# Which engine reads the score banks: ACT copies both halves of the scores to SBUF, and DVE adds and bounds them there

## Chip, cores and metric

One core of a Trainium2 chip runs the whole kernel. The metric is the device time of one execution in microseconds; 901.45 us is the median of three runs before the change.

## The reference, cut to what matters

One layer of a streaming encoder block on 1024 positions of width 1024: a norm, one input projection, attention in a window, a gated mixing branch, two output projections, a residual and a last norm. The change lies in the attention alone:

```
s = jnp.einsum('bnqhgd,bnkhd->bhgnqk', qc, kb,
               preferred_element_type=jnp.float32) * (HEAD_DIM ** -0.5)
...
m = jnp.maximum(jnp.max(s, axis=-1, keepdims=True), sink)
p = jnp.exp(s - m)
denom = jnp.sum(p, axis=-1, keepdims=True) + jnp.exp(sink - m)
o = jnp.einsum('bhgnqk,bnkhd->bnqhgd', p / denom, vb.astype(jnp.float32))
```

There are 16 heads of 64 channels, two groups of keys, chunks of 64 positions, and 192 keys that a query sees (fewer at the start of the sequence). All in float32.

## The kernel before, in words

**Product matmuls.** Nearly all of TensorE's work is large products, each done with seven half-size products in place of eight (`gemm_pair`), and each float32 operand split into a high and a low part. ACT casts the high part (`split`, L176), DVE subtracts to get the low part (L177), and three matmuls of 128x512 make up each step (`product`, L357). A product of 12 matmuls ends in a bank of PSUM (`ps_mm`, `ps_o` or `ps_tp`); ACT copies some of these into tiles `x` (L375, L379, L382, L527), DVE adds others (L387, L392, L396). Weights come in as `wr` over the sync queue (L212) or as sums `s`; DVE makes further sums of them (L257 to L260).

**Attention between them.** The attention is written as a generator that is advanced by one or two parts behind each product (the `hook` calls in `gemm_pair`), from about 303 to 580 us. There are 32 steps: two key groups, eight tiles of 128 queries, two parities of heads. A step has these parts: turn the weights of the step before last (transposes L1481 into `ps_tp`, split L176/L177 into `pT`, L1500/L1502 into `pTb`), scores of the chunks c = 0, scores of the chunks c = 1, values of an earlier step (L1516, L1521 into `ps_o`, out by L1529 on ACT and L1530 on DVE).

**The scores.** For each c there is a pair of score matmuls (L1433), one for each i. Queries and keys are split in high and low parts too, stacked along the contraction and the columns, so that one matmul of 384 columns gives both halves of the sum for 192 keys: `sc[:, 0, :]` and `sc[:, 1, :]`. The result lies in one of the two banks `ps_sc`. Then ACT copies the second half into the tile `sl` (L1441; two buffers), DVE adds the first half from PSUM to `sl`, writes the sum to `pr`, and keeps its minimum and the bound of the sink in `nmax` (L1442, one custom instruction and a short one that reads its accumulator), and ACT takes the exponential with the row's sum (L1452). After both c, DVE and ACT work out the denominators (L1458 to L1462) and scale (DVE L1467 for c = 0, ACT L1469 for c = 1).

There are 128 score matmuls, 64 pairs: 112 of 384 columns, eight of 256 and eight of 128. A pair needs both banks, so it waits for the last reader of the pair before.

**Order.** Each engine runs its instructions in a fixed order. It is not written out by hand: a scheduler in the framework places every instruction when the program is built, by its own estimates of when operands and banks come free. A change of one reader therefore moves instructions on other engines.

Of the kernel before, what the change touches and what calls it, by code (L numbers as in the profile page):

```python
# [24 lines left out]
F32 = mybir.dt.float32  # L25
# [5 lines left out]
P = 128  # L31
# [21 lines left out]
def hybrid_tile(  # L53
# [16 lines left out]
    nc = tc.nc  # L70
# [12 lines left out]
    def bank(tag, dt=F32):  # L83
        return psum.tile([P, 512], dt, name=nm("ps_" + tag), tag="ps_" + tag, bufs=2)

    def mtile(shape, dt, tag, bufs, pool=None):
        return (pool or main).tile(shape, dt, name=nm(tag), tag=tag, bufs=bufs)
# [1315 lines left out]
    def atile(shape, dt, tag, bufs):  # L1403
        return mtile(shape, dt, tag, bufs, pool)
# [3 lines left out]
    def small():  # L1408
        return mtile([P, 2, 2], F32, "sm", 12, aheads)

    def window_of(t, c):

        return (64 * c, 64 * c + 192) if t else (P, P + 64 * (c + 1))

    def softmax_stage(g, t, par, qt):

        kt = keys[g, t][0]
        q_of = qt[:].rearrange("p i (q c) -> p c (i q)", c=2)  # L1420
        nmax, sums = small(), small()
        n_pr[0] += 1
        pr = mtile([P, 2, 384], F32, f"pr{n_pr[0] % 2}", 1, aheads if n_pr[0] % 2 else weights_pool)
        held_in = {}
        sinks_of = (v[:, 4 * g + par : 4 * g + par + 3 : 2] for v in (sink_sb, nsink_sb))
        sk, nsk = sinks_of
        for c in range(2):
            lo, hi = window_of(t, c)
            wide = hi - lo
            scores = []  # L1430
            for i in range(2):
                sc = bank("sc")[:, 0 : 2 * wide].rearrange("p (f k) -> p f k", f=2)
                nc.tensor.matmul(  # L1433
                    sc, q_of[:, c, i * P : (i + 1) * P], kt[:, :, lo:hi], start=True, stop=True
                )
                scores.append(sc)
            for i, sc in enumerate(scores):
                at = 192 * (1 - c) if t else P * (1 - c)
                held_in[c, i] = v = pr[:, i, at : at + wide]
                by_low = atile([P, 192], F32, "sl", 2)[:, 0:wide]  # L1440
                nc.scalar.copy(by_low, sc[:, 1, :])  # L1441
                nc.vector.tensor_tensor_reduce(  # L1442
                    v,
                    sc[:, 0, :],
                    by_low,
                    1.0,
                    nsk[:, i : i + 1],
                    op0=ALU.add,
                    op1=ALU.min,
                    accum_out=nmax[:, c, i : i + 1],  # L1450
                )
                nc.scalar.activation(  # L1452
                    v, v, AF.Exp, bias=nmax[:, c, i : i + 1], scale=-1.0, accum_out=sums[:, c, i : i + 1]
                )
            if c == 0:
                yield
        es = small()
        nc.vector.tensor_add(es[:], sk.unsqueeze(1).broadcast_to([P, 2, 2]), nmax[:])  # L1458
        nc.scalar.activation(es[:], es[:], AF.Exp)
        nc.vector.tensor_add(es[:], es[:], sums[:])  # L1460
        inv = small()
        nc.vector.reciprocal(inv[:], es[:])  # L1462
        for c in range(2):
            for i in range(2):
                v = held_in[c, i]
                if c == 0:
                    nc.vector.tensor_scalar_mul(v, v, inv[:, c, i : i + 1])  # L1467
                else:
                    nc.scalar.mul(v, v, inv[:, c, i : i + 1])  # L1469
        held.append(pr)  # L1470
        yield
# [66 lines left out]
    def attention():  # L1538
# [14 lines left out]
        for n, step in enumerate(steps):  # L1553
            if n >= 2:
                weigh(n - 2)
                yield
            halves = softmax_stage(*step, qT.pop(0))
            next(halves)
            yield
            next(halves)  # L1560
            if n + 2 < len(steps):
                qT.append(query_stage(*steps[n + 2]))
            if n in (0, 2):
                value_loads(*tiles[n // 2])
            yield
            if n >= 3:
                value(n - 3)
                yield
# [419 lines left out]
    for p in range(4):  # L1988
# [93 lines left out]
        wide = HALF // 2  # L2082
# [98 lines left out]
```

## Time and profile before

| what | value |
|---|---|
| median of 3 runs (lowest to highest) | 901.45 us (901.11 to 903.2) |
| the profiled execution's own time | 901.43 us |
| its span | 899.6 us |
| mean granted TensorE clock | 0.998 |
| instructions | 13022 |
| PE / weight loads / DVE / ACT / POOL busy | 98% / 81% / 76% / 62% / 17% |
| score copy on ACT, L1441 | 128 |
| add and bound on DVE, L1442 | 128, busy 46.7 us |
| exponential on ACT, L1452 | 128, busy 55.9 us |
| score matmuls, L1433 | 128, busy 42.7 us |

The engines are PE (TensorE's matmuls), PEld (its weight loads, which overlap matmuls), DVE, ACT, POOL and SP. An arrow `out<-in` names the tiles that an instruction writes and reads. In tables of waits and groups, what stands behind an idle time is the instruction that ended it. The profiler models when a matmul ends, and successive matmuls overlap, so a stall is read better from the distance of two starts than from gaps between bars.

### The profile page before, as it was taken

The page shows a single profiled execution, that of the slowest core. Times are in us where ns is not written, and L with a number is a line of the kernel's source. Part 1 is how long each engine was busy: PE and PEld are TensorE (multiplying, and loading weights), DVE is VectorE, ACT ScalarE, POOL GpSimd, SP SyncE. Part 2 cuts the span into 40 slices and gives each one's busy share as a digit, 9 for nine tenths or more (in the row PEclk, how much of TensorE's full clock was granted, in tenths as well). Part 3 has the DMA queues.
Part 4 walks back from the last instruction along what each step waited for, and adds up shares of the span by engine and source line. Part 5 has one row for each costly group of instructions (what it writes and reads, how often), then busy time and mean ns, then how long its engine had stood idle before and what let it go on. Part 6 is the DMA issues. An engine that isn't in the chain of part 4 may idle for free.

```text
span 899.6 us, 13022 instructions
## 1 busy us (share of the span) xinstructions
PE 885.8 (98%) x4117; PEld 731.1 (81%) x4117; DVE 686.9 (76%) x1362; ACT 562.2 (62%) x1189; POOL 152.9 (17%) x218
## 2 busy tenths in 40 slices
PE   9999999999999999999999999999999999999997
PEld 6888888888888787888878787888888888888886
DVE  7879966666685778988777888757796478479886
ACT  7875533334445488888778787855586376367443
POOL 3322222212030010111211011100121122110012
PEclk9999999999999999999999999999999999999999
DMA  9998887958778676887776689979899789998523
GB/s 333 220 283 211 271 199 162 182 161 275 249 244 285 190 193 174 215 194 186 163 223 196 224 252 210 241 277 382 289 292 391 282 229 250 314 293 282 190 101 133
DMA packets 130961, 212.38 MB, mean 236 GB/s; under 512 B 12779, under 2 KB 59371, under 8 KB 130893
## 3 DMA queue, kind: packets, MB, share of 16 engines
q1 hardware_dynamic: 108280, 148.36, 49.3%
q0 software_dynamic: 22464, 62.93, 31.2%
q8 instruction: 32, 0.52, 0.2%
q14 instruction: 37, 0.30, 0.1%
q10 hardware_dynamic: 148, 0.27, 0.1%
HBM read 146.37 MB, written 86.11 MB: 258 GB/s over the span
## 4 chain that ended last, share of the span: by engine, by line
PE 77%; DVE 9%; ACT 5%; DMA 4%; issue 3%; SPq 1%; POOL 0%; ACTq 0%; DVEq 0%
PE ps_mm L357 34%; PE ps_o L357 19%; PE ps_tp L357 7%; PE ps_sc L357 3%; PE ps_tp L788 2%; PE ps_o L788 2%; PE ps_mm L788 2%; DMA wr<-in_w_dram 2%; PE ps_sc L1433 2%; PE ps_tp L1104 2%; ACT pr L1452 1%; DVE pr L1442 1%; DVE pTb L1502 1%; PE ps_sc L788 1%; PE ps_tp L1481 1%
## 5 line engine op out<-in xcount | busy, mean ns | idle before, releaser
L176 ACT CAST wh<-s 128x1024 fp32r<-128x1024 f32 (+1 forms) x79 | 79.3, 1005 | 78.5 <-PE ps_mm L357 30.3
L177 DVE TENSOR_TENSOR wl<-wr,wh 128x512 fp32r<-128x512 f32 (+1 forms) x77 | 72.1, 938 | 63.8 <-ACT wh L176 62.9
L177 DVE TENSOR_TENSOR wl<-s,wh 128x1024 fp32r<-128x1024 f32 (+1 forms) x79 | 92.6, 1172 | 11.9 <-ACT wh L176 11.9
L176 ACT CAST wh<-wr 128x512 fp32r<-128x512 f32 (+1 forms) x77 | 63.1, 821 | 61.0 <-PE ps_mm L357 33.4
L1452 ACT ACTIVATE pr<-pr,sm 128x192 f32<-128x192 f32 (+2 forms) x128 | 55.9, 439 | 24.2 <-DVE sm L1442 23.9
L1442 DVE CUSTOM_DVE_ANT_0 pr<-ps_sc,sl,nsink_sb 128x192 f32<-128x192 f32 (+2 forms) x128 | 46.7, 401 | 16.7 <-ACT sl L1441 15.8
L357 PE MATMUL ps_o<-T_t1h,wh 128*128 128x512 f32 x148 | 57.9, 391 | 0.0
L357 PE MATMUL ps_o<-T_t1h,wl 128*128 128x512 f32 x148 | 57.8, 390 | 0.0
L357 PE MATMUL ps_o<-T_t1l,wh 128*128 128x512 f32 x148 | 57.6, 389 | 0.0
L357 PE MATMUL ps_mm<-T_b11h,wh 128*128 128x512 f32 x140 | 55.0, 393 | 0.0
L357 PE MATMUL ps_mm<-T_t3h,wh 128*128 128x512 f32 x140 | 54.9, 392 | 0.0
L357 PE MATMUL ps_mm<-T_t3h,wl 128*128 128x512 f32 x140 | 54.7, 391 | 0.0
L357 PE MATMUL ps_mm<-T_b11l,wh 128*128 128x512 f32 x140 | 54.7, 391 | 0.0
L357 PE MATMUL ps_mm<-T_t2h,wh 128*128 128x512 f32 x140 | 54.7, 390 | 0.0
L357 PE MATMUL ps_mm<-T_t2h,wl 128*128 128x512 f32 x140 | 54.6, 390 | 0.0
L357 PE MATMUL ps_mm<-T_b11h,wl 128*128 128x512 f32 x140 | 54.6, 390 | 0.0
L357 PE MATMUL ps_mm<-T_t3l,wh 128*128 128x512 f32 x140 | 54.6, 390 | 0.0
L357 PE MATMUL ps_mm<-T_t2l,wh 128*128 128x512 f32 x140 | 54.5, 389 | 0.0
L357 PE MATMUL ps_mm<-T_t4h,wh 128*128 128x512 f32 x136 | 53.5, 393 | 0.0
L357 PE MATMUL ps_mm<-T_t4h,wl 128*128 128x512 f32 x136 | 53.1, 391 | 0.0
L357 PE MATMUL ps_mm<-T_t4l,wh 128*128 128x512 f32 x136 | 53.0, 390 | 0.0
L1433 PE MATMUL ps_sc<-k,q 128*128 128x384 f32 (+2 forms) x128 | 42.7, 376 | 5.5 <-DVE sm L1442 4.9
(425 smaller groups left out, 2451.6 us busy)
## 6 DMA issues: line engine op xcount, KB each, us to landing
wr<-in_w_dram SPq DMA_DIRECT2D x86, 256.0 KB
sums<-in_w_dram POOLq DMA_DIRECT2D x20, 512.0 KB, 7.1
s<-sums SPq DMA_DIRECT2D x20, 512.0 KB
q_hl<-qhl SPq DMA_DIRECT2D x16, 512.0 KB
q<-q_hl SPq DMA_DIRECT2D x64, 128.0 KB
y_dr<-x POOLq DMA_DIRECT2D x28, 256.0 KB, 6.4
g<-in_w_dram POOLq DMA_DIRECT2D x12, 512.0 KB, 6.1
wr<-in_w_dram SPq DMA_DIRECT2D x11, 512.0 KB
```

Source lines behind the costliest of these rows:

```text
L176: hi_of.append(nc.scalar.copy(hi, src))
L177: lo_of.append(nc.vector.tensor_sub(lo, src, hi.bitcast(F32)))
L357: nc.tensor.matmul(acc, lt, rt, start=fresh and k == 0 and n == 0, stop=k == 3 and n == 2, skip_group_check=True,)
L788: mm = nc.tensor.matmul(acc[:], lt, rt, start=fresh and k == 0 and n == 0, stop=stops and k == 3 and n == terms[-1], skip_group_check=True,)
L1104: nc.tensor.matmul(pm[:, t * P : (t + 1) * P], xh[:, half * 4 + t, g * P : (g + 1) * P], bias[-1][1][:, g % 4, :], start=True, stop=True,)
L1433: nc.tensor.matmul(sc, q_of[:, c, i * P : (i + 1) * P], kt[:, :, lo:hi], start=True, stop=True)
L1442: nc.vector.tensor_tensor_reduce(v, sc[:, 0, :], by_low, 1.0, nsk[:, i : i + 1], op0=ALU.add, op1=ALU.min, accum_out=nmax[:, c, i : i + 1],)
L1452: nc.scalar.activation(v, v, AF.Exp, bias=nmax[:, c, i : i + 1], scale=-1.0, accum_out=sums[:, c, i : i + 1])
L1481: nc.tensor.transpose(dst, pr[:, i, block * P : block * P + width], ident[:])
L1502: nc.vector.tensor_sub(b[c][sides[1 - c]], pt[sides[c], 0:256], b[c][sides[c]].bitcast(F32))
```

## The change

`sl` gets room for both halves; ACT copies the whole bank's 384 columns into it (256 or 128 at the start of the sequence), and DVE's operation takes both inputs from `sl`. Nothing else in the source changes.

```diff
-                by_low = atile([P, 192], F32, "sl", 2)[:, 0:wide]
-                nc.scalar.copy(by_low, sc[:, 1, :])
+                two = atile([P, 2, 192], F32, "sl", 2)[:, :, 0:wide]
+                nc.scalar.copy(two, sc)
                 nc.vector.tensor_tensor_reduce(
                     v,
-                    sc[:, 0, :],
-                    by_low,
+                    two[:, 0, :],
+                    two[:, 1, :],
                     1.0,
                     nsk[:, i : i + 1],
```

The bank `ps_sc` then has ACT's copy as its only reader, and the scheduler places score matmuls differently. On TensorE, at the product that runs around 418 us of the profile (into the bank ps_mm_4066, by the form T_t3), the pair of score matmuls into ps_sc_4243 and ps_sc_4245 stood inside the product:

```order
 L357 MATMUL ps_mm_4066<-T_t3l_755,wh_4045 128x512
-L1433 MATMUL ps_sc_4243<-k_3922,q_4027 128x384
 L357 MATMUL ps_mm_4066<-T_t3h_754,wl_4046 128x512
-L1433 MATMUL ps_sc_4245<-k_3922,q_4027 128x384
 L357 MATMUL ps_mm_4066<-T_t3h_754,wh_4045 128x512
```

Now both stand ahead of that product, right behind the one before:

```order
 L357 MATMUL ps_o_4223<-T_b21h_142,wl_3897 128x512
+L1433 MATMUL ps_sc_4243<-k_3922,q_4027 128x384
+L1433 MATMUL ps_sc_4245<-k_3922,q_4027 128x384
 L357 MATMUL ps_mm_4066<-T_t3h_754,wh_4045 128x512
 L357 MATMUL ps_mm_4066<-T_t3l_755,wh_4045 128x512
```

The pair moved up by eight product matmuls. The next pair of the same kind, into ps_sc_4341 (around 426 us), moved by five in the same way, and of the 64 pairs 25 begin earlier than before, by one to twelve product matmuls; the others begin at their old place.

On ACT, at the same place of the program, the copies grow and a few neighbours change places (wide copies L1441, the exponentials L1452, the cast of turned weights L176 and L1500, the output copy L1529):

```order
-L1441 COPY sl_4247<-ps_sc_4243 128x192
-L1441 COPY sl_4251<-ps_sc_4245 128x192
+L1441 COPY sl_4247<-ps_sc_4243 128x384
+L1441 COPY sl_4251<-ps_sc_4245 128x384
+L176 CAST pT_4295<-ps_tp_4290 128x512
 L1529 COPY aT_4268<-ps_o_4269 64x2x4x64
 L1452 ACTIVATE pr_789_4210,sm_4209<-pr_789_4210,sm_4208 128x192 x2
-L176 CAST pT_4295<-ps_tp_4290 128x512
```

A pair of copies still stands behind the exponentials of the pair before, and one cast moved ahead of the next exponentials. On DVE the rows of L1442 keep their order and name `sl` as their only tile input beside the bounds; adds next to them change places by one or two. On the sync queue some loads of queries, keys and weights change places; the queue of POOL is the same.

## The prediction

> **What bounds the kernel now.** I read the page's busy shares first, then busy time by stretch, then who waits for whom, then a short piece of the timeline, and last the chain of waits.
>
> ```profile
> PE 885.8 (98%) x4117; PEld 731.1 (81%) x4117; DVE 686.9 (76%) x1362; ACT 562.2 (62%) x1189; POOL 152.9 (17%) x218
> ```
>
> TensorE bounds the whole, and 899.6 - 885.8 = 13.8 us of idle is all that the page grants. The change touches only the score rows, which run from 303 to 580 us. The table of busy time has that stretch and, as a clean one, 600 to 700 us. Its columns are length, then busy time and instructions of PE, PEld, DVE, ACT and POOL, then the granted clock, the DMA share and GB/s.
>
> ```profile
> 303.00:580.00 277.00, 271.46 (x1310) 222.08 (x1308) 224.66 (x646) 223.47 (x680) 38.46 (x49) 1.00 0.76 204
> 600.00:700.00 100.00, 100.00 (x443) 82.81 (x442) 75.74 (x88) 64.29 (x85) 15.50 (x26) 1.00 0.99 344
> ```
>
> The clock is full in both, so it explains nothing. In the score stretch PE idles 5.5 us, DVE is busy 81% and ACT 81% (53.5 us free). The table of waits, from 300 to 600 us, for PE and its weight loads, and from 303 to 580 us for ACT:
>
> ```profile
> PE ps_sc L1433 <- DVE sm L1442: 4.9, 13, 0.9
> PEld ps_sc L1433 <- DVE sm L1442: 14.7, 25, 1.0
> ACT pr L1452 <- DVE sm L1442: 23.9, 23, 2.2
> ACT wh L176 <- PE ps_mm L357: 7.3, 9, 2.0
> ACT aT L1529 <- PE ps_o L1521: 5.4, 9, 1.0
> ACT pr L1469 <- DVE sm L1462: 4.0, 6, 1.5
> ```
>
> PE waits there for one thing: a score matmul needs a bank of ps_sc (there are two), and the last reader of a bank is DVE's add-and-bound at L1442. The loss lies between 4.9 us (matmul idle, understated because the modelled end of one matmul lies beyond the start of the next) and 14.7 us (weight loads). One case in the timeline shows how much is real (start, duration, engine, line, in us):
>
> ```profile
> 415.83 0.53 ACT L1441 COPY sl<-ps_sc 128x192 f32<-128x192 f32 x2
> 418.00 0.39 PE L357 MATMUL ps_mm<-T_t3h,wh 128*128 128x512 f32 x1
> 418.22 0.39 PE L357 MATMUL ps_mm<-T_t3l,wh 128*128 128x512 f32 x1
> 418.45 0.42 DVE L1442 CUSTOM_DVE_ANT_0 pr<-ps_sc,sl,nsink_sb 128x192 f32<-128x192 f32 x1
> 418.93 0.19 PEld L1433 LDWEIGHTS ps_sc<-k,q 128*128 128x128 f32 x1 [0.74 <-DVE sm L1442]
> 418.94 0.45 PE L1433 MATMUL ps_sc<-k,q 128*128 128x384 f32 x1 [0.32 <-DVE sm L1442]
> 419.22 0.39 PE L357 MATMUL ps_mm<-T_t3h,wl 128*128 128x512 f32 x1
> 419.81 0.52 ACT L1441 COPY sl<-ps_sc 128x192 f32<-128x192 f32 x2
> 423.85 0.53 ACT L1441 COPY sl<-ps_sc 128x192 f32<-128x192 f32 x2
> 425.66 0.39 PE L357 MATMUL ps_mm<-T_t4l,wh 128*128 128x512 f32 x1
> 426.02 0.45 PE L1433 MATMUL ps_sc<-k,q 128*128 128x384 f32 x1
> 426.31 0.40 PE L357 MATMUL ps_mm<-T_t4h,wl 128*128 128x512 f32 x1
> ```
>
> Running freely, a 512-column matmul starts every 0.22 to 0.23 us (418.00, 418.22), so 384 columns take about 0.17. At 418.94 the step is 0.72 and the next one 0.28: (0.72 - 0.23) + (0.28 - 0.17) = 0.60 us lost, against 0.74 shown at the weight load. At 426.02 it is (0.36 - 0.23) + (0.29 - 0.17) = 0.25 us lost, with no gap shown on PE at all. So I take three quarters of 14.7 us, about **11 us**, as what PE really loses to late banks.
>
> **The change part by part.** *ACT copies both halves.* Rows by form, each with its count, total us and mean ns:
>
> ```profile
> L1441 ACT COPY sl<-ps_sc 128x192 f32<-128x192 f32 x112 | 29.4, 312 | 0.0
> L1441 ACT COPY sl<-ps_sc 128x128 f32<-128x128 f32 x8 | 1.6, 253 | 0.0
> L1441 ACT COPY sl<-ps_sc 128x64 f32<-128x64 f32 x8 | 1.4, 208 | 1.5 <-DVE s L257 1.5
> L375 ACT COPY x<-ps_mm 128x512 f32<-128x512 f32 x12 | 6.9, 578 | 4.7 <-PE ps_mm L357 4.7
> ```
>
> From 192 to 512 columns a copy out of PSUM grows by 266 ns, 0.83 ns a column. The 384-column copy has no row; by this slope it takes 312 + 192 x 0.83 = 472 ns, 160 more. Bounds by the neighbours' slopes: 0.70 (64 to 128 columns) gives 135 more, 0.92 (128 to 192) gives 177. I take 160, since its two rows enclose 384. The sum: 112 x 0.160 + 8 x 0.112 (128 to 256) + 8 x 0.045 (64 to 128) = **19.2 us more of ACT** (15 to 21), 0.32 us for each pair of copies. ACT's busy share then rises from 0.81 to 242.7 / (277 - 11) = 0.91 if PE loses nothing.
>
> *DVE reads both inputs from SBUF.* The rows of plain adds on 512 columns, first with a PSUM input, then with both in SBUF, then the operation itself and a one-input operation in SBUF of its width:
>
> ```profile
> L177 DVE TENSOR_TENSOR pT<-ps_tp,pT 128x512 fp32r<-128x512 f32 x28 | 19.2, 687 | 7.5 <-ACT pT L176 7.4
> L259 DVE TENSOR_TENSOR s<-wr,wr 128x512 f32<-128x512 f32 x10 | 6.8, 683 | 0.0
> L1442 DVE CUSTOM_DVE_ANT_0 pr<-ps_sc,sl,nsink_sb 128x192 f32<-128x192 f32 x112 | 42.2, 414 | 15.4 <-ACT sl L1441 14.5
> L1467 DVE TENSOR_SCALAR pr<-pr,sm 128x192 f32<-128x192 f32 x56 | 15.4, 318 | 0.8
> ```
>
> Where the input lies moves an add by 4 ns of 687. I take the operation as unchanged at 414 ns. The far end is 318 ns, 128 x 0.096 = 12.3 us less of DVE; the other end is +4 ns, 0.5 us more. [...]
>
> *The bank is free sooner.* ACT's copy becomes its only reader. At 415.83 the pair of copies is done by 416.36, by 416.7 when longer; DVE began to read only at 418.45. The order of instructions uses this: the score pair of 418.94 stands 8 product matmuls earlier, that of 426.02 five. 8 x 0.23 = 1.8 us earlier is 418.94 - 0.49 - 1.8 = 416.6 for a bank whose first copy ends at 415.83 + 0.47 = 416.3: 0.3 to spare. For the pair of 426.02: 425.9 less 1.15 less the 0.6 already won is 424.1, against 423.85 + 0.47 = 424.3, so about 0.2 us of a new wait. No DMA is added, but on the sync queue loads of queries and weights change places, mostly by one. An issue takes 0.59 us:
>
> ```profile
> 400.92 0.59 SPq L1380 DMA_DIRECT2D q<-q_hl  x1
> ```
>
> PE waits for no DMA here (its one row stands above), though the chain passes a weight load twice (the share of 6.5% in a row below). Two places in the queue would be 1.2 us either way; I take nothing.
>
> *What ACT's longer copies push.* Behind each pair of copies stand on ACT the exponentials, the split of the next weights and the copies of x out of ps_mm and ps_o. The cover is ACT's idle time, 53.5 us in the stretch, of which 27.9 is waiting for DVE and most of the rest for PE. Where ACT has no idle time the 0.32 us goes through. The chain of waits shows such a place (start, us, what):
>
> ```profile
> 383.51 0.42 ACT sl L1441 x2
> ...
> 428.08 0.89 ACT wh L176
> ...
> 436.61 0.42 ACT sl L1441 x2
> ...
> 439.96 0.52 ACT wh L176
> ...
> 445.11 0.28 DVE pr L1442
> 445.46 0.60 PE ps_sc L1433 x2
> ...
> 515.86 0.42 ACT sl L1441 x2
> ...
> 542.07 0.42 ACT sl L1441 x2
> ```
>
> From 428 to 440 the chain lies nearly all on ACT, then on DVE, and comes back to PE through the bank. The copies at 383, 515 and 542 us lie in three more such stretches. Each of the four holds one pair of copies on the chain and about two beside it, 0.32 to 0.96 us, 1.3 to 3.8 us together. I take 3, near the top, since the pairs beside the chain have little idle time next to them. For new waits of PE behind copies, like the 0.2 us worked out above, I take 2 us, which is 0.3 us at one in ten of the 64 pairs. **The sum: -11 + 3 + 2 = -6 us.** The profiled execution took 901.43 us (span 899.6 and 1.8 around it), 0.02 below the median of the three runs; 901.4 - 6 = **895.5 us**.
>
> **The rivals.** *The wait changes its owner (no change).* PE would wait for ACT's copies as long as it did for DVE. For it: at 426.02 the margin is gone, and the copies stay behind exponentials that still wait for DVE (23.9 us). Against it: in the two cases shown the first copy ends 1.7 and 2.6 us before DVE let the bank go (424.3 for 426.02, 416.3 for 418.93). The time is 901 us.
>
> *ACT becomes the bound (slower).* Place: the ring of copies, DVE's bound and exponentials, in which ACT and DVE are each busy four fifths of the time and hand over in a fixed order. If the idle time cannot be used, because ACT waits for DVE (27.9 us) at points that move along with it, the 19.2 us lands on the ring, PE runs out of its lead, and the time is 901.4 + 19.2 - 11 = 909.6 us; with no bank won, 920.6. It decides once ACT absorbs less than 8 of its 19.2 us. Against it: most waits of ACT directly follow longer work of DVE or PE, into which a later ACT simply sinks. [...]
>
> *DVE's operation shrinks too.* At 318 ns the sum gains what of L1442 is on the chain. The line of shares from the chain of waits between 330 and 440 us:
>
> ```profile
> by line: PE ps_mm L357 20.9%; PE ps_o L357 12.5%; PE ps_sc L1433 6.7%; DMA wr<-in_w_dram 6.5%; issue 6.1%; ACT pr L1452 5.0%; DVE pr L1442 4.8%; PE ps_tp L1481 3.8%; DVE pTb L1502 3.6%; DVE wl L177 2.9%; ACT wh L176 2.6%; PE ps_o L1516 2.5%
> ```
>
> Scaled to the stretch, 4.8% of 277 us is 13 us; a quarter off (96 of 414 ns) is 3 us, so 892.5 us. The two adds speak against it. That the change does not do what it says is excluded: in its order of instructions DVE's rows name sl alone.
>
> **How the numbers follow.** Forecast, PE's bank waits mostly gone: 0.47. DVE shorter as well: 0.08. No change: 0.23. ACT the bound: 0.22. A measurement of this kernel tells about 0.3% (2.7 us) from no change, so faster has 0.55, same 0.23 and slower 0.22. The forecast's own range is 887 (all 14.7 us won) to 898.7. With the case of no change and the smaller half of the slower one, up to 908, about 0.15 is left out.
>
> **What would show it.** Right, if in the profile after the waits of PE and PEld at L1433 name ACT's copy and fall below 5 us together, the copy stands near 472 ns, DVE's operation near 414, and PE idles about 2 us between 303 and 580. Wrong, if the waits at L1433 stay near 14.7 us under ACT's name, if product matmuls (L357) or transposes (L1481) begin to wait for ACT or DVE, or if DVE's operation comes out far from 414 ns.

## The result, and the profile after the change

The changed kernel takes 904.58 us, the median of five runs (904.42 to 906.35), against 901.45 us (901.0 to 903.2): ratio 1.0034, 95% interval 1.002 to 1.0049. It is 3.1 us slower; the forecast was 6 us faster. The profiled execution has a span of 903.3 us, against 899.6.

The busy line of the page after:

```profile
PE 888.1 (98%) x4117; PEld 730.6 (81%) x4117; DVE 688.6 (76%) x1362; ACT 579.3 (64%) x1189; POOL 151.7 (17%) x218
```

ACT has 17.1 us more, DVE 1.7 more. The two instructions that the change touches, by form, after:

```profile
L1441 ACT COPY sl<-ps_sc 128x384 f32<-128x384 f32 x112 | 47.2, 473 | 0.0
L1442 DVE CUSTOM_DVE_ANT_0 pr<-sl,nsink_sb 128x192 f32<-128x192 f32 x112 | 42.8, 416 | 16.4 <-ACT sl L1441 15.5
```

The copy takes 473 ns and the bound 416. Both prices were right (472, and 414 unchanged). So the loss has to lie in the waits or in the order of instructions. PE's and its weight loads' waits after, from 300 to 600 us (what waited, for whom, total us, times, longest):

```profile
PEld ps_sc L1433 <- ACT sl L1441: 12.1, 33, 1.6
PEld ps_o L1516 <- DVE x L387: 6.0, 9, 1.1
PE ps_o L1516 <- DVE x L387: 2.8, 7, 0.7
PE ps_sc L1433 <- ACT sl L1441: 2.7, 6, 1.2
```

The scores' waits carry ACT's name, as they should, but at the weight loads they fell only from 14.7 to 12.1 us, and at the matmuls from 4.9 to 2.7. New is a wait that the table of before does not have: the value matmul L1516 waits for DVE's addition L387.

The stage repeats a round: one product pair (seven products) with the attention steps between. L387 stands in it once, so its first and last start give the round. The view of this line between 380 and 575 us, of before and then of after (count, duration shortest/median/longest in ns, first and last start, form):

```profile
L387 DVE TENSOR_TENSOR x<-x,ps_o x7: 681/682/684, 392.7 to 551.3; 128x512 f32<-128x512 f32 x7
```

```profile
L387 DVE TENSOR_TENSOR x<-x,ps_o x7: 680/682/684, 394.5 to 554.5; 128x512 f32<-128x512 f32 x7
```

Before, a round is (551.3 - 392.7) / 6 = 26.43 us; after, (554.5 - 394.5) / 6 = 26.67. About ten rounds at 0.24 us more are 2.4 of the 3.1 us. Over all ten rounds, from the first L387 of the stage to the eleventh, it is 264.06 us (315.19 to 579.25) against 261.33 (314.73 to 576.06), 2.7 us more. The round is used for all kernels below, since it does not contain what happens ahead of the stage and behind it. It also leaves out the stage's first three rounds, so where those matter the ten rounds are given beside it.

### The profile page after: what moved, and what is told of

Its sections match the earlier page's. It is cut to its first block, busy times and chain, and to the rows that moved or that the text cites. A ratio compares the mean times of both kernels' runs of the same rounds, so it can differ in the third digit from the quotient of the medians.

```text
span 903.3 us, 13052 instructions
## 1 busy us (share of the span) xinstructions
PE 888.1 (98%) x4117; PEld 730.6 (81%) x4117; DVE 688.6 (76%) x1362; ACT 579.3 (64%) x1189; POOL 151.7 (17%) x218
## 4 chain that ended last, share of the span: by engine, by line
PE 78%; DVE 7%; ACT 6%; DMA 5%; issue 3%; SPq 1%; POOL 0%; ACTq 0%; DVEq 0%
PE ps_mm L357 33%; PE ps_o L357 20%; PE ps_tp L357 7%; DMA q<-q_hl 3%; PE ps_sc L357 3%; PE ps_tp L788 2%; PE ps_o L788 2%; PE ps_mm L788 2%; PE ps_tp L1104 2%; ACT pr L1452 2%; PE ps_sc L1433 2%; PE ps_sc L788 1%; PE ps_o L1516 1%; PE ps_tp L1481 1%; DVE pTb L1502 1%
## 5 line engine op out<-in xcount | busy, mean ns | idle before, releaser
L176 ACT CAST wh<-s 128x1024 fp32r<-128x1024 f32 (+1 forms) x79 | 79.4, 1006 | 71.6 <-PE ps_mm L357 26.2
L177 DVE TENSOR_TENSOR wl<-wr,wh 128x512 fp32r<-128x512 f32 (+1 forms) x77 | 72.0, 936 | 62.4 <-ACT wh L176 62.4
L177 DVE TENSOR_TENSOR wl<-s,wh 128x1024 fp32r<-128x1024 f32 (+1 forms) x79 | 92.8, 1175 | 11.4 <-ACT wh L176 11.4
L176 ACT CAST wh<-wr 128x512 fp32r<-128x512 f32 (+1 forms) x77 | 63.0, 820 | 57.3 <-PE ps_mm L357 34.3
L1452 ACT ACTIVATE pr<-pr,sm 128x192 f32<-128x192 f32 (+2 forms) x128 | 56.0, 440 | 23.2 <-DVE sm L1442 22.5
L1442 DVE CUSTOM_DVE_ANT_0 pr<-sl,nsink_sb 128x192 f32<-128x192 f32 (+2 forms) x128 | 47.3, 403 | 17.6 <-ACT sl L1441 16.7
L1441 ACT COPY sl<-ps_sc 128x384 f32<-128x384 f32 (+2 forms) x128 | 51.4, 453 | 1.3 <-DVE s L257 1.3
```

The lines of the kernel that those rows point to most:

```text
L176: hi_of.append(nc.scalar.copy(hi, src))
L177: lo_of.append(nc.vector.tensor_sub(lo, src, hi.bitcast(F32)))
L1441: nc.scalar.copy(two, sc)
L1442: nc.vector.tensor_tensor_reduce(v, two[:, 0, :], two[:, 1, :], 1.0, nsk[:, i : i + 1], op0=ALU.add, op1=ALU.min, accum_out=nmax[:, c, i : ...
L1452: nc.scalar.activation(v, v, AF.Exp, bias=nmax[:, c, i : i + 1], scale=-1.0, accum_out=sums[:, c, i : i + 1])
```

## The experiments

The experiments were compared with the kernel before on the same chip, whose median was 901.96 to 902.67 us there. The last two columns are the first and last start of L387 and the round that follows (six rounds lie between; five in f3 and x2). A round is from one profiled execution, a ratio from all runs.

| kernel | median us | ratio [95%] | L387 from, to | round us |
|---|---|---|---|---|
| before | 901.45 | 1 | 392.7, 551.3 | 26.43 |
| after | 904.58 | 1.0034 [1.002, 1.0049] | 394.5, 554.5 | 26.67 |
| e1 long copy alone | 902.05 | 1.0002 [0.9993, 1.0011] | 393.9, 551.9 | 26.33 |
| e2 after, pairs held back | 904.69 | 1.0038 [1.0025, 1.0051] | 397.0, 556.8 | 26.63 |
| e3 free release | 900.33 | 0.9987 [0.9978, 0.9995] | 393.6, 550.7 | 26.18 |
| e4 first chunk only | 901.83 | 0.9999 [0.999, 1.0008] | 392.9, 550.6 | 26.28 |
| f1 after, cast first | 904.16 | 1.0018 [1.0009, 1.0027] | 396.1, 554.7 | 26.43 |
| f2 before, cast first | 901.22 | 0.9991 [0.9982, 1.0] | 394.1, 552.0 | 26.32 |
| f3 after, sum on GpSimd | 928.73 | 1.0292 [1.0272, 1.0311] | 402.3, 546.3 | 28.8 |
| f4 after, scaling on GpSimd | 901.46 | 0.9992 [0.9982, 1.0002] | 395.4, 551.8 | 26.07 |
| h1 after, value in ps_tp | 903.81 | 1.002 [1.0011, 1.0028] | 394.3, 553.3 | 26.50 |
| h2 before, value in ps_tp | 901.5 | 0.999 [0.9981, 0.9999] | 392.4, 550.5 | 26.35 |
| h3 before, scaling on GpSimd | 901.82 | 0.9998 [0.9989, 1.0007] | 394.2, 551.3 | 26.18 |
| k1 after, more ACT | 905.62 | 1.0035 [1.0022, 1.0048] | 395.7, 555.1 | 26.57 |
| k2 before, more ACT | 902.05 | 0.9994 [0.9985, 1.0002] | 392.8, 551.5 | 26.45 |
| k3 after, both reliefs | 902.15 | 1.0001 [0.9991, 1.0011] | 394.7, 551.9 | 26.20 |
| k4 before, both reliefs | 903.64 | 1.0018 [1.0009, 1.0026] | 394.3, 553.3 | 26.50 |
| x1 change in the old order | 902.67 | 1.0007 [0.9998, 1.0016] | 394.1, 552.4 | 26.38 |
| x2 before in the new order | 954.97 | 1.0586 [1.057, 1.0602] | 406.4, 562.6 | 31.24 |
| x3 x1, L387 earlier | 905.73 | 1.0036 [1.0023, 1.005] | 393.1, 553.5 | 26.73 |

### The two parts of the change: e1 to e4

The first theory was that the change's two sides fight: the bank comes free early (a gain), and ACT's longer copies eat it (a loss). The rival was that the moved instructions cost the time.

**e1**, the long copy alone. DVE reads its first input from PSUM again:

```diff
-                    two[:, 0, :],
+                    sc[:, 0, :],
```

> ACT copies all 384 columns, but DVE still reads the first half from PSUM, so the bank is let go by DVE as before and the order of score matmuls stays about as before. This prices ACT's longer copies alone. Theory ring (ACT and DVE hand over in a fixed order with little real slack, and longer copies lengthen that ring): 6 to 12 us over the kernel before. Theory order (the copies sink into ACT's idle time, and what cost time in the changed kernel is its new order on PE, with value matmuls waiting for DVE's L387): within 2 us of the kernel before.

902.05 us, no difference. The longer copies alone cost nothing, so the theory of a cost on ACT by itself fell.

**e2**, the changed kernel with each score matmul held in PE's order behind the bound (L1442) that let its bank go before:

```diff
+                if bounds:
+                    after(mm, bounds.pop(0))
...
-                nc.vector.tensor_tensor_reduce(
+                bound = nc.vector.tensor_tensor_reduce(
...
+                bounds.append(bound)
```

> The changed kernel, with each score matmul held in the program order behind DVE's operation of the pair before (an order without a wait), so that PE meets the score matmuls about where it did before the change, while the bank is let go by ACT. Theory order: the waits of value matmuls (L1516) for L387 go and the gain by free banks is left, 895 to 899 us. Theory ring: the place of the score matmuls hardly matters, 902 to 906 us, with the PE waits elsewhere.

904.69 us, inside what the theory of a ring had expected (902 to 906). But the links gave an order between the two, with other changes on ACT, so this was no clean return to the old order (x1 below is), and the run decides little.

**e3**, the release alone: ACT copies 192 columns as before, DVE adds a tile of zeros in place of the first half of the scores, which this kernel leaves out.

```diff
+    none = mtile([P, 192], F32, "none", 1, pool)
+    nc.gpsimd.memset(none[:], 0.0)
...
-                    sc[:, 0, :],
+                    none[:, 0:wide],
```

> Leaves out the first half of the scores: ACT copies 192 columns as before, and DVE adds a tile of zeros in SBUF in place of the PSUM half. So the bank is let go by ACT, the order on PE is that of the changed kernel, and ACT does no more than before. Theory ring: 3 to 9 us faster than the kernel before, the gain that the prediction expected and that the longer copies ate. Theory order: no gain or slower than before, 901 to 905 us.

900.33 us, so the early bank without any cost on ACT is worth 0.0013 x 902 = 1.2 us, not 11. This lies between the two theories' ranges. Its waits from 303 to 584 us say why (the file has two lines more, so L1518 is the value matmul):

```profile
PEld ps_o L1518 <- DVE x L387: 10.4, 10, 1.4
PE ps_o L1518 <- DVE x L387: 6.2, 9, 1.0
```

The score waits are nearly gone (2.4 us left at the weight loads), and PE waits a little further on for L387.

**e4**, the whole change for the first chunk (c = 0) only:

```diff
+                if c == 0:
+                    nc.scalar.copy(two, sc)
+                    first = two[:, 0, :]
+                else:
+                    nc.scalar.copy(two[:, 1, :], sc[:, 1, :])
+                    first = sc[:, 0, :]
```

> The change for the first chunk of each step alone (c = 0), whose bank the next pair waits for in the same step; the order on PE is that of the changed kernel, and ACT's added time is half, about 9.6 us. Theory ring: about half of the copies' price comes off, 2 to 6 us faster than the changed kernel, 898 to 902 us. Theory order: as slow as the changed kernel, 903 to 906 us.

901.83 us, no difference: half of the longer copies, with half of the early release, cost nothing.

### The place of the cast, and reliefs: f1 to f4

Neither part alone is slow and both together are, so the next theory was a loop through ACT and DVE that sets the length of a round, with PE waiting now for one of its links, now for another. Its links are DVE's reciprocal (L1462), ACT's scaling (L1469), ACT's cast of the next weights (L176, 512 columns), DVE's low half `wl` (L177), four sums and the turned weights' low halves, DVE's bounds (L1442), and then L387 behind them. Two stretches of the timeline hold the same place of the program, of before (start, duration, engine, line, in us):

```profile
386.06 0.80 ACT L1469 ACTIVATE pr<-pr,sm 128x192 f32<-128x192 f32 x2 [0.50 <-DVE sm L1462]
386.77 0.60 ACT L176 CAST wh<-wr 128x512 fp32r<-128x512 f32 x1
...
387.40 0.59 ACT L382 COPY x<-ps_mm 128x512 f32<-128x512 f32 x1
387.41 0.69 DVE L177 TENSOR_TENSOR wl<-wr,wh 128x512 fp32r<-128x512 f32 x1 [0.85 <-ACT wh L176]
...
392.01 0.42 DVE L1442 CUSTOM_DVE_ANT_0 pr<-ps_sc,sl,nsink_sb 128x192 f32<-128x192 f32 x1
...
392.69 0.68 DVE L387 TENSOR_TENSOR x<-x,ps_o 128x512 f32<-128x512 f32 x1
...
393.65 0.63 PE L1516 MATMUL ps_o<-pT,v 128*128 128x512 f32 x2
```

and of after:

```profile
387.26 0.80 ACT L1469 ACTIVATE pr<-pr,sm 128x192 f32<-128x192 f32 x2 [0.50 <-DVE sm L1462]
...
388.09 0.58 ACT L382 COPY x<-ps_mm 128x512 f32<-128x512 f32 x1
...
388.57 0.62 ACT L176 CAST wh<-wr 128x512 fp32r<-128x512 f32 x1
...
389.23 0.69 DVE L177 TENSOR_TENSOR wl<-wr,wh 128x512 fp32r<-128x512 f32 x1 [1.48 <-ACT wh L176]
...
393.83 0.42 DVE L1442 CUSTOM_DVE_ANT_0 pr<-sl,nsink_sb 128x192 f32<-128x192 f32 x1
...
394.51 0.68 DVE L387 TENSOR_TENSOR x<-x,ps_o 128x512 f32<-128x512 f32 x1
...
395.25 0.73 PE L1516 MATMUL ps_o<-pT,v 128*128 128x512 f32 x2 [0.45 <-DVE x L387]
```

Two things are to be seen. Before, ACT casts first and copies `x` (L382) afterwards; after, it is the other way round, DVE starts 0.63 us later behind the scaling (1.48 against 0.85 of waiting), and everything down to L387 with it. And the value matmul starts 0.28 us behind L387's end before (393.65 - 393.37), but 0.06 after (395.25 - 395.19): it now waits for L387. Counted in the order of instructions, the cast stands ahead of L382 in nine of ten rounds before and in four of ten after.

**f1** and **f2**, the cast ahead of that copy in all rounds of the stage, in the kernel after and in the kernel before:

```diff
-        pace[0] = nc.scalar.copy(x12[:], acc)
-        split_next()
+        pace[0] = (split_next() if in_attention[0] else None, nc.scalar.copy(x12[:], acc))[1]
+        None if in_attention[0] else split_next()
```

> The changed kernel, but during the score rows ACT's cast of the next weight block (L176) is put ahead of the copy of x12 (L382) in all nine places, where the changed kernel has it behind in five. Theory 'cast place': the loop of one product round goes from ACT's scaling over the cast to seven DVE operations, to the addition at L387 and to the value matmul, and a cast behind the 512-column copy lengthens it by 0.47 us; this kernel gets 5 x 0.47 = 2.4 us back: 901.5 to 902.5. Theory 'longer copies in the loop' (the place of the cast is of no account, the 0.32 us of each pair of copies is what counts, as ACT is without slack there): it stays within 1 us of 904.6.

> The kernel before, with the same edit (the cast ahead of the copy of x12 in all nine places; before, it is behind in one). Theory 'cast place': little to win, and the cast is still behind the scaling in five places: 900.5 to 902. Theory 'longer copies': 901.5, no difference. Both the same here: it is the control for the edit itself, and a time over 903 would say that the edit does something else than move the cast.

f1 took 904.16 us, ratio 1.0018: between the two theories' numbers, though its interval overlaps that of after. Its round is 26.43, that of before. But this holds for the six rounds from 396 us on alone: its ten rounds take 264.11 us (315.34 to 579.45), as long as after's 264.06. Its profiled execution (905.23 us, 1.1 over the median) loses 1.7 us at the start of the stage (below), about half of it inside these ten rounds. So what the cast's place is worth is not shown. f2 is 0.8 us under before, at the limit of what can be told.

**f3**, the sum s3 (L259) on GpSimd during the stage:

```diff
-            free.append(nc.vector.tensor_add(s3, a11, a21))
+            free.append((nc.gpsimd if in_attention[0] else nc.vector).tensor_add(s3, a11, a21))
```

> The changed kernel, but during the score rows the sum s3 = a11 + a21 of a weight block (L259, 0.68 us on DVE, once in a product round) runs on GpSimd. It is one of the seven operations that DVE does between ACT's cast and the addition at L387. Theory 'one loop through ACT, DVE and the value matmul sets the round': up to 0.68 us less in each of ten rounds, at most the 5 us that PE idles there: 899 to 901. Theory 'DVE has slack there and only ACT's queue counts': 904, no difference. Against both: if GpSimd's addition comes late for the transposing transfer of s3, it is slower than 905.

928.73 us, far over both theories' numbers. The expectation's third case, over 905, covers it, but the way is another: DVE itself slows down. The same place in the timeline of f3:

```profile
396.11 2.68 DVE L257 TENSOR_TENSOR s<-wr 128x512 f32<-128x512 f32 x1
396.35 1.89 POOL L259 TENSOR_TENSOR s<-wr,wr 128x512 f32<-128x512 f32 x1
...
403.04 0.72 PE L1516 MATMUL ps_o<-pT,v 128*128 128x512 f32 x2 [2.54 <-DVE x L387]
```

While GpSimd adds, DVE's own addition takes 2.68 us in place of 0.69. DVE's run of operations got longer by 2.68 - 0.69 - 0.68 = 1.3 us instead of shorter, PE waits 2.54 us for L387, and the round grows by 2.1 us. It is a relief that turned into a load, and it fits the theory: what is added to DVE's run comes through to PE.

**f4**, the scaling of the second chunk (L1469) on GpSimd:

```diff
-                    nc.scalar.mul(v, v, inv[:, c, i : i + 1])
+                    nc.gpsimd.tensor_scalar_mul(v, v, inv[:, c, i : i + 1])
```

> The changed kernel, but the scaling of the second chunk's probabilities (L1469, 56 of 0.47 us, 26 us of ACT) runs on GpSimd. Theory 'one loop': two scalings of a pair go out of ACT's part of the loop, up to 0.9 us a round, bounded by the 5 us that PE idles: 899 to 901.5, and ACT's cast follows DVE's sums at once. Theory 'cast place': the cast may still stand behind the copy of x12, but without the scalings ahead of it, 901 to 903. If GpSimd is slow at it (over 1 us each), the transposes at L1481 wait and the time is over 905.

901.46 us with the shortest round of all, 26.07. Its ten rounds take 259.44 us (316.22 to 575.66), 1.9 less than before. The profiled execution is the slowest of this kernel's twelve (904.55 us, 3.1 over its median): its stage ends 0.4 us earlier than that of before, but its span is 3.2 us longer, so it loses 3.6 us behind the stage. Whether the other executions do so too is not known. In the chain of waits between 588 and 614 us of f4 stand

```profile
590.79 4.53 DMA at_dr<-aT
...
597.46 14.94 DMA bq<-z_dr
612.41 0.03 ACT bq L1750
```

The attention's last output is written, 3 MB are read, and ACT, in its fixed order, waits for them 3 us ahead of the copies that PE needs next. PE waits 1.3 us for the first of them (L375); in the kernel before it waits for nothing there.

### One bank further: h1 to h3

If what holds PE back were only the bank of `ps_o` that L387 lets go, then a value matmul in another bank should win what the scores could not. **h1** (after) and **h2** (before):

```diff
-        po = bank("o")
+        po = bank("tp")
```

**h3** is f4's edit on the kernel before.

> The changed kernel, but the value matmul (L1516) writes to a bank of the transposes (ps_tp) and not of ps_o, so it needs no longer the bank that DVE's addition at L387 lets go. Theory 'shadow' (once the score bank is free early, PE waits for the bank of L387, 0.2 to 0.3 us behind): the 6.0 us of weight-load waits at L1516 go, the score banks stay early, and the time falls by 2 to 5 us: 899.5 to 902.5. Rival 'ACT's queue' (the 19 us of longer copies delays all that follows on ACT, whatever bank PE waits for): other waits, on ACT's copies of scores or on the splits of the transposes, take their place, 903.5 to 905.5. Rival 'transposes are next': with three users of two ps_tp banks the transposes (L1481) wait for DVE's L1530 or L1502, over 906.

> The kernel before, with the same edit alone. Theory 'shadow': before, the score bank (let go by L1442, just ahead of L387 on DVE) is the one waited for, L387 stands behind it; taking L387 out wins nothing that lasts, since the waits at L1433 stay near 14 us: 900.5 to 902.5. Rival 'ACT's queue': the same, 901 to 902. If it is faster by over 2 us, the bank of L387 was waited for before too, and the account of before is wrong.

> The kernel before, but the scaling of the second chunk's probabilities (L1469) runs on GpSimd, as in the run on the changed kernel that came out 0.7 us below the kernel before. It tells how much of that was the change's. Theory 'the change pays once ACT is relieved' : the kernel before gains less, 901 to 903, more than the changed kernel with the same edit (901.5). Theory 'scaling alone': the kernel before gains the same 3 us, 898 to 899.5.

h1 took 903.81 us, what the rival expected. Its waits from 303 to 584 us:

```profile
PEld ps_sc L1433 <- ACT sl L1441: 7.5, 25, 1.6
PEld ps_tp L1481 <- DVE aT L1530: 4.8, 11, 0.8
PEld ps_tp L1516 <- DVE pT L177: 4.3, 8, 0.8
```

L387 is out of the list, and DVE's L177 and L1530 are in it: 16.6 us in three lines, where after had 18.1 in two. h2 came out at 0.999 and h3 at no difference. By the side of f4 (0.9992), h3 (0.9998) says that with ACT's scalings gone the change costs nothing.

### ACT's time, and both reliefs: k1 to k4

**k1** and **k2** put about the change's own cost on ACT once more, into the kernel after and the kernel before:

```diff
+                if c == 0:
+                    nc.scalar.copy(atile([P, 192], F32, "un", 1)[:, 0:wide], two[:, 1, :])
```

(`by_low` for `two[:, 1, :]` in k2.) **k3** and **k4** have both reliefs, f4's and h1's edits, on after and before.

> The changed kernel with one more copy on ACT for each score tile of the first chunk (192 columns, SBUF to SBUF, into a tile that nobody reads): 64 copies, about 0.3 us each, 17 to 19 us of ACT in the stage, as much as the change itself added; the bank is not held longer. Theory 'ACT's time' (with the score bank let go by ACT, the stage has no cover left on ACT, and its added time comes through in part): 3 to 8 us over the changed kernel, 907.5 to 912.5. Theory 'order' (the 3 us come from the places in ACT's queue alone): within 1.5 us of the changed kernel, 903 to 906.

> The kernel before with the same 64 copies more on ACT. With DVE as the last reader the longer copies alone cost nothing (902.05 against 901.96). Theory 'ACT's time': ACT has cover there, 901.5 to 903.5. Theory 'order': the order on ACT is that of before, so no more than 1 us, 901.5 to 902.5. Over 905 would say that ACT's cover in the kernel before was nearly used up too, and that the longer copies cost nothing only by their place.

> The changed kernel with both reliefs: the scaling of the second chunk on GpSimd (26 us off ACT) and the value matmul in a bank of ps_tp (not behind L387). Alone they gave 901.5 and 903.8. Theory 'shadows' (each bank wait hides the next, and all but the loop's own work go when ACT has time): the waits at L1433 and L1516 fall below 4 us together and the time is 897 to 900.5, less what the transfer behind the stage takes back (0.7 to 2.3 us at 611 us). Theory 'PE has nothing left to win': 900.5 to 902, and new waits at L1481 or L1516 for DVE.

> The kernel before with both reliefs: the control. Alone they gave 901.8 and 901.5. Theory 'shadows': the score bank, let go by L1442, stays the wait that counts, 900.5 to 902, so k3 is 1 to 4 us below it, and the change is worth having once ACT is relieved. Theory 'PE has nothing left': 900.5 to 902, equal to k3.

The 56 wide ones of the added copies in k1:

```profile
L1443 ACT COPY un<-sl 128x192 f32<-128x192 f32 x56 | 19.8, 354 | 0.2
```

19.8 us more of ACT, and k1 stands at 1.0035 where after stands at 1.0034; k2 at 0.9994. So ACT's time as such is not the cause, and that theory fell; at the place that I read, around 394 us, ACT still waits 1.63 us for DVE's bound behind the added copies. k3 came out at 902.15 us, against 'shadows': L1433 and L1516 wait little, but the transposes (L1481) wait 9.8 us at the weight load for DVE's L1530. k4 (903.64 us, where both theories had at most 902) is slower than either relief alone; the reliefs don't add up. k1, k3 and k4 also have another order of instructions than the kernels they start from, which left the order to be tried by itself.

### Order and operations apart: x1 to x3

The change moves 328 places on PE, 135 on ACT, 71 on DVE and 87 on the sync queue, 621 in all (the 32 in x2's expectation are no count of these lists). Both kernels have the same instructions in the same program order, so the one's order can be laid on the other. **x1** has the operations of after, each engine in exactly the order of before; **x2** the operations of before in the order of after. Every neighbour in a list is linked without a wait:

```diff
+        ins = list(nc.cur_bb.bb.instructions)
+        for row in ORDER:
+            for a, b in zip(row, row[1:]):
+                tc.add_manual_dep(
+                    ins[b],
+                    ins[a].name,
+                    mybir.DependencyInfo(mybir.DependencyClass.NoSync, mybir.DependencyReason.DATA),
+                    reason="order",
+                )
```

> The changed kernel's instructions, each engine's and the sync queue's in exactly the order of the kernel before (held by order-only links between neighbours; no wait is added). Theory 'order': the operations themselves cost nothing; with the bank let go earlier and PE asking for it where it did before, PE's waits at L1433 fall and the time is 898 to 901.5. Theory 'operations' (the longer copies or the release through ACT cost time in any order): 903.5 to 906.

> The instructions of the kernel before in the order of the changed kernel (32 places of 3,900 differ). Theory 'order': the score pairs stand earlier among the products while their banks are still let go by DVE, so it is slower than before, 904 to 910, with the waits at L1433 for DVE grown. Theory 'operations': 901 to 903, as before.

x1 took 902.67 us, ratio 1.0007 with 1 inside the interval: the operations cost nothing that can be told, and win nothing either. The other 2.4 us ((1.0034 - 1.0007) x 902) are the order's. Its waits from 303 to 584 us:

```profile
PEld ps_o L1516 <- DVE x L387: 12.4, 10, 1.9
PE ps_o L1516 <- DVE x L387: 8.5, 10, 1.5
PEld ps_sc L1433 <- ACT sl L1441: 1.8, 4, 0.7
...
PE ps_sc L1433 <- ACT sl L1441: 0.6, 2, 0.3
```

This is the clearest table of the study. In the same order, the score waits fell from 14.7 and 4.9 us to 1.8 and 0.6, just as forecast, and the value matmul, which did not wait before, waits 12.4 and 8.5. The stage takes as long: ten rounds are 261.89 us in x1 (315.24 to 577.13), 261.33 before. The timeline of x1 at the place shown above:

```profile
387.44 0.80 ACT L1469 ACTIVATE pr<-pr,sm 128x192 f32<-128x192 f32 x2 [0.50 <-DVE sm L1462]
388.15 0.60 ACT L176 CAST wh<-wr 128x512 fp32r<-128x512 f32 x1
...
393.25 0.34 PE L1433 MATMUL ps_sc<-k,q 128*128 128x384 f32 x1
...
393.38 0.42 DVE L1442 CUSTOM_DVE_ANT_0 pr<-sl,nsink_sb 128x192 f32<-128x192 f32 x1
...
394.81 0.73 PE L1516 MATMUL ps_o<-pT,v 128*128 128x512 f32 x2 [0.75 <-DVE x L387]
```

The score matmul runs at 393.25, ahead of the bound it used to wait for; 1.5 us later PE stands still for L387, which DVE does behind that bound.

x2 took 954.97 us, far over the 904 to 910 expected: with DVE as the last reader, score pairs that stand up to twelve matmuls earlier wait for it 34.4 us on PE:

```profile
PE ps_sc L1433 <- DVE sm L1442: 34.4, 19, 3.2
```

The new order fits the new release alone.

**x3** is x1 with L387 five operations earlier on DVE in ten rounds, behind `pT` and ahead of L260, L1502 twice and L1442 twice.

> The changed instructions in the order of before, but in ten rounds DVE does the addition at L387 right behind the low half of the transposed probabilities (L177 pT), ahead of L260, L1502 twice and L1442 twice, 2.3 us earlier; its product is done by then. Theory 'one wait behind the other': the waits at L1516 (8.5 us at the matmul, 12.4 at the weight load in x1) fall below 2 and 4 us, about 0.9 us is won in each of nine rounds less 0.3 that the bounds behind it come later, 3 to 6 us in the stage; of it 1 to 2 us go back at 611 us behind the stage: 897 to 900.5. Rival 'the loop through ACT and DVE sets the round': the waits come back at L1433, L1481 or L357 with the same sum, 901.5 to 903.5.

905.73 us, slower than x1 by 2.6 us by the ratios: the rival was right about the loop, and even it expected too little. The same place in x3:

```profile
388.77 0.80 ACT L1469 ACTIVATE pr<-pr,sm 128x192 f32<-128x192 f32 x2 [0.50 <-DVE sm L1462]
...
393.13 0.68 DVE L387 TENSOR_TENSOR x<-x,ps_o 128x512 f32<-128x512 f32 x1
...
394.56 0.63 PE L1516 MATMUL ps_o<-pT,v 128*128 128x512 f32 x2
...
395.31 0.42 DVE L1442 CUSTOM_DVE_ANT_0 pr<-sl,nsink_sb 128x192 f32<-128x192 f32 x1
...
395.77 0.45 ACT L1452 ACTIVATE pr<-pr,sm 128x192 f32<-128x192 f32 x1 [2.13 <-DVE sm L1442]
...
396.66 0.83 ACT L1441 COPY sl<-ps_sc 128x384 f32<-128x384 f32 x2
...
397.17 0.45 PE L1433 MATMUL ps_sc<-k,q 128*128 128x384 f32 x1 [1.09 <-ACT sl L1441]
```

The value matmul no longer waits. In its place the score matmul does, where x1 had 1.8 us of such waits:

```profile
PEld ps_sc L1433 <- ACT sl L1441: 12.8, 18, 1.5
```

The bound comes 0.6 us later behind the scaling (395.31 - 388.77 = 6.54, in x1 393.38 - 387.44 = 5.94), the exponentials wait for it, ACT's copies stand behind the exponentials, and the next score matmul waits for the copies. ACT's release of the bank was never free of DVE: it hangs on DVE's bound by way of ACT's queue.

So the stretch from DVE's reciprocal (end of L1462) to its next bound (start of L1442) can be read off the timelines for seven rounds each:

| kernel | mean us | its rounds | round us |
|---|---|---|---|
| x1 | 5.81 | 6.04, 5.22, 6.04, 5.47, 6.66, 5.22, 6.04 | 26.38 |
| before | 5.82 | 6.05, 5.22, 6.04, 5.47, 6.66, 5.24, 6.04 | 26.43 |
| after | 6.10 | 6.66, 6.64, 5.09, 5.95, 5.09, 6.63, 6.66 | 26.67 |
| x3 | 6.41 | 6.63, 5.81, 6.64, 6.07, 7.26, 5.81, 6.64 | 26.73 |
| f4 | 5.46 | 5.41, 5.44, 5.41, 4.99, 5.41, 6.15, 5.41 | 26.07 |

After has four rounds of 6.63 to 6.66 us, four of the five here that have the cast behind L382 (the fifth has 5.95), where before has one. The stretch is 0.28 us longer on average and the round 0.24. In x3 it is 0.6 longer in every round than in x1, and the round 0.35.

It is not all: k1 (5.89 us, round 26.57), k4 (5.76, 26.50), e1 (5.25, 26.33), e3 (5.95, 26.18) and h1 (6.33, 26.50) don't fit this line, so other parts of the order count as well. So it is argued, not shown, that this stretch sets the round. Which moved instructions make up the 2.4 us of order stays open; the cast's place is one candidate.

## Why the prediction was wrong, point by point

- **The prices of the operations** were right: copy 473 ns for 472, bound 416 for 414.
- **The term of -11 us is the step that failed.** It took three quarters of the weight loads' bank waits as time that PE gets back. x1 shows those waits nearly gone (from 14.7 to 1.8 us) and the time not won. Each hid another wait of the same loop: right behind L1442 on DVE stood L387, for whose bank the value matmul had only 0.28 us to spare in the round shown, and in x1 it waits 12.4 us for it. e3 puts what the early bank is worth at 1.2 us with no cost on ACT; with it, x1 shows no gain (1.0007).
- **The 0.3 us to spare for a copy** was worked out from ACT's place in the profile of before. ACT's copies stand behind exponentials that wait for DVE's bound (22.5 us of such waits after, 23.9 before). The rival of no change named that, and I set it aside for two places where the copy happened to be early. x3 shows it at work.
- **The +3 us for ACT's longer copies** look like the 3.1 us that were measured, but that is chance. The copies alone cost nothing (e1), as much ACT again costs nothing (k1, k2). The cost came with the order: 2.4 us by x1. By the medians f1 gives back 1.4 of it by the cast's place, but the intervals overlap and its ten rounds show no gain.
- **The +2 us for new waits** had ACT's copies alone as what PE would wait for. The new wait was for DVE's L387, 6.0 us at the weight loads of the value matmul after the change.
- **The moved instructions** were priced by the score pairs and two queue places alone. That ACT's cast fell behind a copy of 0.6 us in five more rounds was in the order of instructions, on the chain that I had quoted (ACT wh L176 stands in it twice), and had no term. What it costs by itself is not shown (f1).
- **The rivals.** No change (901) is what the operations do in the old order. ACT as the bound (909.6) had the sign, but not the mechanism, for k1 speaks against it. The marks set for the profile after decided well: the waits at L1433 came to 12.1 + 2.7 = 14.8 us under ACT's name, where below 5 was the mark for right. What the marks did not name was a wait of the value matmul. (In the sum, 901.4 - 6 is 895.4, not 895.5.)

## What to carry to other kernels

A wait in the table was not worth its time here, because another stood right behind it. Before taking a wait out, look what the engine that ends it does next, and who needs that. Where a scheduler sets the order, price every instruction that moves on the loop, also on engines that the edit doesn't touch; a small edit's order can be told from its operations by laying the old order on the new operations. No version here clearly beats the kernel before: the lowest that computes all, h2, is at 0.999 [0.9981, 0.9999].

## What the runs showed of the hardware that was not expected

**In f1 the clock fell to half behind 2.04 us without a matmul.** In f1's profiled execution PE waited 2.04 us ahead of the score matmul at 312.51 us, in after 1.23 us at the same place. The table of busy time of f1 (the clock is the number behind POOL):

```profile
310.00:312.00 2.00, 0.48 (x3) 0.05 (x1) 0.93 (x2) 0.09 (x1) 0.00 (x0) 1.00 0.46 165
312.00:314.00 2.00, 1.49 (x6) 1.29 (x7) 1.50 (x6) 1.61 (x8) 0.00 (x0) 0.88 0.15 38
314.00:316.00 2.00, 2.00 (x7) 1.61 (x7) 2.00 (x9) 1.34 (x3) 0.00 (x0) 0.50 0.76 218
316.00:318.00 2.00, 2.00 (x8) 1.59 (x8) 1.97 (x9) 1.49 (x9) 0.00 (x0) 0.77 0.83 256
```

2 x (0.12 + 0.50 + 0.23) = 1.7 us are lost; after the shorter wait the clock stayed at 1.00. In f3 the wait of 2.54 us at 403 us is followed by a clock of 0.50 and 0.65 in the next two stretches of 2 us. That is 2 x (0.50 + 0.35) = 1.7 us again. By an estimate it does not follow each time: PE has nine waits for L387 there (20.8 us together, 2.9 the longest), at 1.7 us each 15 us of clock, and f3's mean clock of 0.97 over 303 to 580 us is a loss of about 277 x 0.03 = 8 us. So a gap of 2.04 us was enough once; what decides it is not shown.

**DVE's addition took 2.68 us beside GpSimd's, in place of 0.69.** In f3 a 128x512 addition on GpSimd (L259) took 1.6 us on average, and in the round shown above DVE's L257 ran beside it. Over all 23 of L257 the mean is 944 ns, in after 686: (944 - 686) x 23 = 5.9 us, as much as three rounds at 2.0. In f4, with the scaling on GpSimd (848 ns on average), DVE is busy 219.99 us with 608 instructions between 326 and 584 us, in after 210.62 with 601.
